# An eight-core streaming trunk rescheduled: narrower halo, packed weights, a stacked depthwise convolution, norms inside the stages

## Chip, cores and metric

The kernel runs on the 8 cores of one Trainium2 chip, each core working on half of one prompt and on one sample stream. The time is that of the slowest core, in device microseconds (us). Some executions fall into a slower state in which the cores of one die show a lower granted TensorE clock than the others (in the slowest run of the changed kernel, 4371.96 us, 0.844 to 0.853 on one die and 0.972 to 0.974 on the other); only fast runs are compared here, and where a profile fell into the slow state, a core of the undisturbed die is read and named. The engines are PE (TensorE; PEld its weight loads), DVE (VectorE), ACT (ScalarE), POOL (GpSimd) and SP (SyncE).

## The reference, cut to what matters

```python
def trunk(x, conv_past, ...):                 # D = 1024, 4 layers
    for i in range(DEPTH):
        h = rms_norm(x, norm_mix_g[i])
        if i % 2 == 0:   # gMLP: v normalised per token, mixed over chunks of 128 frames
            z = gelu(h @ w_in + b_in); u, v = z[..., :3072], layer_norm(z[..., 3072:])
            y = (u * (tril(w_s) @ v + b_s)) @ w_out + b_out
        else:            # GLU -> causal depthwise convolution, width 31 -> LayerNorm -> silu -> pointwise
            a = h @ w_pw1 + b_pw1; glu = a[..., :D] * sigmoid(a[..., D:])
            c = silu(layer_norm(depthwise(concat(past, glu)) + b_dw)); y = c @ w_pw2 + b_pw2
        x = x + y
        h = rms_norm(x, norm_ffn_g[i])
        x = x + (silu(h @ w_gate) * (h @ w_up)) @ w_down     # D_FF = 2816
    return rms_norm(x, norm_final_g), conv states, normalised v
```

Four prompts of 4096 frames and eight sample streams of 32 frames. All matmuls run in bf16 with f32 sums.

## The kernel before

Activations lie channels-first: 8 blocks of 128 channels by up to 1184 token columns, in three tiles of up to 416. A core makes two passes over all four layers. The core with the second half of a prompt recomputes the 256 frames before it, the halo. The norms form stages of their own, behind a barrier:

```python
def ffn(layer, tiles):
    P.barrier()
    norm_to_h(tiles, "ffng", layer)      # per tile: 8 squares (ScalarE), 8 ones-matmuls, rsqrt, 8 scalings (VectorE)
    for mb in range(11):
        ...                              # gate/up
    for m in range(KC):
        ...                              # down: all tiles of an output block, then the next block
```

The depthwise convolution multiplies by diagonal 128x128 matrices, which ScalarE builds for every tap, and leaves 7 of the 31 taps of seven channel blocks to VectorE:

```python
mms = [lambda e, k=k, ...: e.matmul(
    ps[:, b, 0:nm], lhsT=(DIAG7[:, k, :] if k < NDVE else DIAG[:, dp, k, :]),
    rhs=PD[:, kc, c0 + k:c0 + k + nm], start=(k == nd), stop=(k == 30)) for k in range(nd, 31)]
...
for k in range(nd):                      # NDVE = 7 taps
    ... P.op("dve", lambda e, ...: e.scalar_tensor_tensor(out=CC[:, kc, ...], in0=PD[:, kc, c0 + k:...],
            scalar=pcol("wdw", ...), in1=CC[:, kc, ...], op0=ALU.mult, op1=ALU.add), ...)
```

And in the gating unit TensorE goes from the v projection to u and mixing at once, so that mixing waits for all of v to be normalised.

## Time and profile before

| | before |
|---|---|
| fast runs | 4489 to 4492 us |
| TensorE busy, idle (core 5) | 4109.5, 379.5 us |
| VectorE, ScalarE busy | 2085.1, 1293.3 us |
| mean granted clock | 0.96 |

TensorE, busy 92% of the span and 83% of the chain that ended last, sets the time: the question for every part of the change is how many columns it takes out of TensorE's stream, and which of its gaps. The prediction shows the lines. One more table of stretches: the four convolutions of this kernel, from the first pointwise 1 matmul to the first FFN matmul (columns: stretch, length, busy time of PE, PEld, DVE, ACT, POOL with counts, granted clock, DMA share, GB/s).

```profile
659.60:879.10 219.50, 196.68 (x1247) 123.51 (x1245) 143.04 (x307) 123.09 (x309) 8.74 (x10) 0.94 0.25 32
1665.40:1865.30 199.90, 176.07 (x1248) 113.37 (x1246) 130.88 (x307) 117.74 (x309) 8.74 (x10) 0.93 0.27 33
2763.90:3016.40 252.50, 219.30 (x1446) 127.98 (x1444) 166.04 (x360) 129.19 (x310) 8.73 (x10) 0.93 0.23 31
3942.60:4196.80 254.20, 221.14 (x1445) 128.53 (x1444) 165.78 (x359) 129.16 (x310) 8.74 (x10) 0.93 0.21 27
```

They take 926.1 us together, of which TensorE is busy 813.2 and idle 113.

### The profile page before, as it was taken

Reading aid. Unit: us, or ns where it says so; the run is one execution under the profiler, and the core shown is the slowest. Engines: PE = TensorE matmul, PEld = TensorE weight load, DVE = VectorE, ACT = ScalarE, POOL = GpSimd, SP = SyncE. Lnnn points to the kernel's source line nnn. Section 1 sums busy time; section 2 is a strip of 40 time slices with the busy share of each in tenths; the row PEclk is TensorE's granted clock in tenths of the full one; section 3 lists DMA queues with packets and bytes.
Section 4 is the critical chain, followed back from the end, with each engine's and each line's share of the span. In section 5 each row is a group of like instructions: output and inputs, shape, how many; then the busy total and the mean of one; then the engine's idle time right before and its main releaser. Section 6 shows DMA issues by size and latency. Waiting matters only on the chain.

```text
span 4489.0 us, 71170 instructions; the slowest of 8 cores (4479.6 to 4489.0 us)
## 1 busy us (share of the span) xinstructions
PE 4109.5 (92%) x25674; PEld 2433.8 (54%) x25674; DVE 2085.1 (46%) x4066; ACT 1293.3 (29%) x2821; POOL 350.1 (8%) x372
## 2 busy tenths in 40 slices
PE   6899999799899999896899999979998999997998
PEld 2465656566466666563355555635544555554554
DVE  4764225622865226523776212762157652148422
ACT  3222225511322126412312222541032121146311
POOL 0000110011001110010000001001100001100000
PEclk9999999899999999898999999989999999998999
DMA  6344573267345563377334455115543445640345
GB/s 122 52 62 59 61 67 39 29 77 79 59 71 68 71 68 39 40 81 140 60 55 67 57 61 67 22 29 67 58 68 49 61 64 65 65 50 1 48 60 82
DMA packets 514118, 273.78 MB, mean 61 GB/s; under 512 B 192944, under 2 KB 508720, under 8 KB 513712
## 3 DMA queue, kind: packets, MB, share of 16 engines
q0 software_dynamic: 489216, 239.10, 44.2%
q1 hardware_dynamic: 24560, 30.14, 2.6%
q8 instruction: 213, 3.49, 0.3%
q14 instruction: 129, 1.06, 0.1%
HBM read 498.48 MB, written 9.80 MB: 113 GB/s over the span
## 4 chain that ended last, share of the span: by engine, by line
PE 83%; DVE 7%; ACT 5%; issue 3%; SPq 1%; DMA 1%; DVEq 0%; ACTq 0%
PE ps L387 29%; PE ps L401 15%; PE ps L451 9%; PE ps L616 8%; PE ps L551 7%; PE ps L673 6%; PE ps L779 5%; ACT SQ L52 4%; DVE BIG L810 2%; PE ps L833 2%; PE ps L572 1%; PE ps L340 1%; SPq L856 1%; DVE BIG L493 1%; DVE FT L582 1%
## 5 line engine op out<-in xcount | busy, mean ns | idle before, releaser
L387 PE MATMUL ps<-hA,RING 128*128 128x384 bf16 (+3 forms) x8448 | 1323.5, 320 | 0.0
L387 PEld LDWEIGHTS ps<-hA,RING 128*128 128x128 bf16 x8448 | 814.9, 98 | 509.5 <-issue 6.9
L394 DVE TENSOR_TENSOR BIG<-ps,FT 128x384 bf16<-128x384 f32 (+2 forms) x528 | 285.1, 541 | 991.3 <-PE ps L387 975.9
L401 PE MATMUL ps<-BIG,RING 128*128 128x384 bf16 (+2 forms) x4224 | 659.5, 319 | 0.0
L52 ACT ACTIVATE FT<-ps 128x384 f32<-128x384 f32 (+4 forms) x556 | 263.6, 477 | 1057.0 <-PE ps L387 1016.8
L401 PEld LDWEIGHTS ps<-BIG,RING 128*128 128x128 bf16 x4224 | 405.9, 98 | 252.3
L52 ACT ACTIVATE SQ<-xA 128x384 bf16<-128x384 f32 (+3 forms) x432 | 181.2, 498 | 819.8 <-DVE xA L405 633.4
L616 PE MATMUL ps<-AUX,RING 128*128 128x384 bf16 (+2 forms) x2304 | 380.9, 326 | 34.3 <-DVE AUX L594 33.2
L551 PE MATMUL ps<-hA,RING 128*128 128x384 bf16 (+2 forms) x2304 | 395.0, 329 | 3.6 <-DVE FT L582 3.6
L451 PE MATMUL ps<-RING,hA 128*128 128x512 bf16 (+1 forms) x1776 | 392.0, 383 | 6.8 <-DVE hA L354 6.8
L779 PE MATMUL ps<-BIG,AUX 128*128 128x384 bf16 (+2 forms) x2388 | 362.1, 313 | 0.7 <-ACT AUX L52 0.7
L405 DVE TENSOR_TENSOR xA<-ps,xA 128x384 f32<-128x384 f32 (+3 forms) x192 | 103.9, 541 | 554.3 <-PE ps L401 554.3
L52 ACT ACTIVATE AUX<-ps,PPS 128x384 bf16<-128x384 f32 (+2 forms) x288 | 165.0, 576 | 612.7 <-PE ps L551 560.3
L616 PEld LDWEIGHTS ps<-AUX,RING 128*128 128x128 bf16 x2304 | 223.8, 98 | 187.2 <-issue 50.5
L810 DVE SCALAR_TENSOR_TENSOR BIG<-BIG,PPS 128x384 f32<-128x384 bf16 (+2 forms) x588 | 301.1, 578 | 38.1 <-ACT BIG L52 38.1
L340 PE MATMUL ps<-SQ,ONES 128*128 128x384 bf16 (+3 forms) x432 | 131.7, 478 | 191.3 <-ACT SQ L52 191.3
L551 PEld LDWEIGHTS ps<-hA,RING 128*128 128x128 bf16 x2304 | 223.3, 99 | 143.6 <-issue 13.8
L451 PEld LDWEIGHTS ps<-RING,hA 128*128 128x128 bf16 (+1 forms) x1776 | 173.0, 99 | 226.0 <-issue 25.8
L779 PEld LDWEIGHTS ps<-BIG,AUX 128*128 128x128 bf16 x2388 | 222.9, 97 | 133.5 <-issue 2.1
L354 DVE SCALAR_TENSOR_TENSOR hA<-xA,PPS,FT 128x384 bf16<-128x384 f32 (+3 forms) x384 | 200.8, 601 | 119.7 <-ACT FT L52 119.7
L673 PE MATMUL ps<-hA,RING 128*128 128x384 bf16 (+2 forms) x1536 | 251.5, 328 | 0.0
L52 ACT ACTIVATE AUX<-IDENTB,PPS 128x128 bf16<-128x128 bf16 x796 | 241.1, 390 | 0.0
(72 smaller groups left out, 2695.7 us busy)
## 6 DMA issues: line engine op xcount, KB each, us to landing
RING<-ffn_w_gate POOLq DMA_DIRECT2D x88, 512.0 KB, 7.9
RING<-ffn_w_up POOLq DMA_DIRECT2D x88, 512.0 KB, 9.8
RING<-ffn_w_down POOLq DMA_DIRECT2D x64, 704.0 KB, 9.5
RING<-sgu_w_in POOLq DMA_DIRECT2D x24, 1024.0 KB, 11.6
RING<-sgu_w_in POOLq DMA_DIRECT2D x32, 768.0 KB, 7.9
RING<-sgu_w_out POOLq DMA_DIRECT2D x32, 768.0 KB, 7.6
RING<-conv_w_pw POOLq DMA_DIRECT2D x32, 512.0 KB, 9.3
RING<-conv_w_pw POOLq DMA_DIRECT2D x8, 1024.0 KB, 10.2
```

The lines of the kernel that those rows point to most:

```text
L52: return self.e.activation(**kw)
L340: P.op("pe", [lambda e, kc=kc, n=n, par=par, b=b: e.matmul(ps[:, b, 0:n], lhsT=ONES[:, :], rhs=SQ[:, par, kc, 0:n], start=(kc == 0), stop= ...
L354: P.op("dve", lambda e, kc=kc, c0=c0, n=n, par=par, tt=tt: e.scalar_tensor_tensor(out=out_fn(kc, tt, c0, n), in0=xA[:, kc, c0:c0 + n], sca ...
L387: P.op("pe", [lambda e, kc=kc, w_=w_, b_=b_, c0=c0, n=n, j=j: e.matmul(ps[:, b_, 0:n], lhsT=w_[:, kc, j * 128:(j + 1) * 128], rhs=hA[:, kc ...
L394: P.op("dve", lambda e, bu=bu, n=n, par=par, mc=mc, c0=c0: e.tensor_tensor(out=A_[:, mc, c0:c0 + n], in0=ps[:, bu, 0:n], in1=FT[:, 4 + par ...
L401: P.op("pe", [lambda e, kc=kc, b=b, c0=c0, n=n, sW=sW: e.matmul(ps[:, b, 0:n], lhsT=sW[:, kc, :], rhs=A_[:, kc, c0:c0 + n], start=(kc == 0 ...
L451: P.op("pe", [lambda e, kc=kc, b=b, cc0=cc0, rows=rows, wv=wv: e.matmul(ps[0:rows, b, :], lhsT=hA[:, kc, cc0:cc0 + rows], rhs=wv[:, kc, :] ...
L551: P.op("pe", [lambda e, kc=kc, b=b, c0=c0, n=n, w_=wus[s], off=off: e.matmul(ps[:, b, 0:n], lhsT=w_[:, kc, off:off + 128], rhs=hA[:, kc, c ...
L616: P.op("pe", [lambda e, kc=kc, b=b, c0=c0, n=n, w_=wos[s], off=off: e.matmul(ps[:, b, 0:n], lhsT=w_[:, kc, off:off + 128], rhs=UG[:, kc, c ...
L673: P.op("pe", [lambda e, kc=kc, w_=w_, b_=b_, c0=c0, n=n, j=j: e.matmul(ps[:, b_, 0:n], lhsT=w_[:, kc, j * 128:(j + 1) * 128], rhs=hA[:, kc ...
L779: mms = [lambda e, k=k, b=b, kc=kc, dp=dp, c0=c0, nm=nm, nd=nd: e.matmul(ps[:, b, 0:nm], lhsT=(DIAG7[:, k, :] if k < NDVE else DIAG[:, dp, ...
L810: P.op("dve", lambda e, k=k, kc=kc, c0=c0, nm=nm: e.scalar_tensor_tensor(out=CC[:, kc, c0:c0 + nm], in0=PD[:, kc, c0 + k:c0 + k + nm], sca ...
```

## The change

It is a new schedule of the same mathematics. The intent: fewer token columns (the prompt is split at frame 2078, so 30 extra frames replace the halo of 256), weights packed by the host so that a partition's row is contiguous, a depthwise convolution in which four taps and 32 channels share the 128 rows, norms folded into the stage before them, and the gating unit's mixing one head behind its u. A stack below is such a set of shifted copies of one channel block; the tail of a convolution is what follows its last depthwise block: LayerNorm, silu, pointwise 2 and the next norm. The core of the diff, cut:

```diff
-    ST_COLS = [(0, 1152), (1152, 1184)]
+TA = [(0, 384), (384, 384), (768, 288)]
+TB = {0: [(0, 384), (384, 384), (768, 256)], 1: [(0, 384), (384, 384), (768, 320)]}
 ...
+            def later(self, tt, c0, n, d1, d2):          # norm of a tile: sum after d1 groups, scaling after d2 more
+                if self.final is None:
+                    h_ready[tt] = False
+                after(d1, lambda: (self.sum(tt, c0, n), after(d2, lambda: self.scale(tt, c0, n))))
 ...
+            ws = [load(6), load(7)]                      # FFN: the last two output blocks tile by tile
+            for tt, (c0, n) in enumerate(tiles):
+                for j in range(2):
+                    down(6 + j, ws[j][1], ws[j][0], tt, c0, n)
+                    ...                                  # squares of the next norm
+                nnorm.later(tt, *nt, 1, 1)
 ...
+            after(2, v_norm)
+            for hd in range(4):
+                for i, (mc, tt) in enumerate(units):
+                    u_group(hd, mc, tt)
+                    if hd > 0:
+                        mix(hd - 1, mc, tt)
 ...
+            def stack(kc, eng="sp"):                     # row r*32+c holds channel q*32+c, shifted by r
+                for r in range(4):
+                    for q in range(4):
+                        P.dma(eng, lambda e, r=r, q=q: e.dma_start(
+                            out=STK.v[r * 32:(r + 1) * 32, i, q, 0:win],
+                            in_=PD.v[q * 32:(q + 1) * 32, kc, r:r + win]), ...)
+                for j in range(8):
+                    for q in range(4):
+                        mms.append(lambda e, j=j, q=q: e.matmul(
+                            ps[q * 32:(q + 1) * 32, b, 0:nm], lhsT=w[:, q * 8 + j, :],
+                            rhs=STK.v[:, i, q, c0 + 4 * j:c0 + 4 * j + nm], start=(j == 0), stop=(j == 7)))
```

## The prediction

> **What bounds the kernel now.** First the states. Four executions took 4978.88, 4490.53, 5246.91 and 4490.70 us; the profiled one is 4490.53, with all eight cores within 0.2% of one another at a mean clock of 0.96. I predict for that fast state, and core 5's trace is the one read. Then the page: TensorE is busy 92% of the span, VectorE 46%.
>
> ```profile
> PE 4109.5 (92%) x25674; PEld 2433.8 (54%) x25674; DVE 2085.1 (46%) x4066; ACT 1293.3 (29%) x2821; POOL 350.1 (8%) x372
> ```
>
> The chain that ended last says the same by line, and the list of TensorE's waits says where the other 380 us are.
>
> ```profile
> PE 83%; DVE 7%; ACT 5%; issue 3%; SPq 1%; DMA 1%; DVEq 0%; ACTq 0%
> ...
> PE ps L340 <- ACT SQ L52: 191.3, 54, 25.9
> PE ps L727 <- DVE SQ L714: 69.3, 8, 13.6
> PE ps L616 <- DVE AUX L594: 33.2, 34, 3.6
> PE ps L572 <- DVE BIG L493: 27.1, 7, 6.1
> ```
>
> The reader is to see two separate things: a stream of matmuls that only fewer or cheaper matmuls can shorten, and a few kinds of gap, the largest being the column sums of each RMS norm (line 340) waiting for ScalarE's squares.
>
> To split the two by stage I read the busy times in stretches that I cut at the stages (here of the first pass: a norm, gate/up of an FFN, pointwise 1 of the convolution, its depthwise part, its LayerNorm; columns: stretch, length, PE, PEld, DVE, ACT, POOL busy, clock, DMA share, GB/s).
>
> ```profile
> 371.00:386.00 15.00, 7.92 (x26) 3.27 (x27) 6.16 (x12) 12.34 (x27) 1.59 (x2) 0.64 0.56 72
> 386.00:559.00 173.00, 173.00 (x1058) 103.83 (x1057) 42.72 (x78) 34.62 (x70) 16.66 (x18) 0.99 0.54 58
> ...
> 659.60:723.00 63.40, 63.40 (x386) 37.86 (x384) 23.96 (x47) 15.21 (x25) 3.49 (x4) 0.98 0.40 51
> 723.00:808.00 85.00, 81.77 (x567) 54.79 (x565) 74.25 (x156) 64.01 (x201) 1.75 (x2) 1.00 0.12 14
> 808.00:854.00 46.00, 33.73 (x208) 21.39 (x209) 33.45 (x83) 32.49 (x56) 0.00 (x0) 0.85 0.00 1
> ```
>
> Dense stages are 100% TensorE at a clock of 0.98 to 1.00; the low mean comes from the gaps (0.64). So matmuls cost what their column count says. From the chain of waits in order of time: 1056 gate/up matmuls of 384 columns in 173.06 us, 163.9 ns each; taking that out of stages of mixed width, 256 columns are 108.1 ns and 416 are 176.3; 432 of 512 in 94.81 us are 219.5 ns; a 128-column one is 79 (66.2 us over 840). I interpolate 288 to 122.5 and 320 to 136.
>
> Adding the chain's stage starts over both passes gives the time before: loads with first norms 101, V projection with its LayerNorm gap 496 (of which PE work 392), gated part u/mix/out 806, FFNs 1980, pointwise 1 251, the rest of the convolutions up to the FFN 675, other norms 151, final norm and store 26. Sum 4486.
>
> [...] the present loads take 98 ns and lie hidden (PEld 54% beside a full PE). [...] "DMA" is 1% of the chain, so bigger pieces alone should buy little. [...]
>
> **The change part by part.** It is nearly a new schedule. I count both kernels' columns from their loop nests.
>
> Fewer token columns. The old one recomputes a 256-column halo in the second half; the new one splits the sequence at frame 2078 and needs 32 extra. FFN columns fall from 8832 to 8448. FFN after: each pass has one tile set 384+384+288 (450.3 ns for a set) and three of 384+384+256 (435.9) or 384+384+320 (463.8), times 528 matmuls per set: 1901 us (was 1980). V: 35 chunks of 128 tokens x 48 x 220 ns = 370, the sample now sharing its chunk (was 392). u and out: 384 matmuls per set = 691; mixing 24 x (32 x 79 + 3 x 60 ns) = 65; together 756. Pointwise 1: 128 per set = 230. Pointwise 2: 64 per set = 115. LayerNorm sums 16 per set = 29. Norm sums 8 per set for 18 norms = 64.
>
> Depthwise convolution. Before: per channel block 24 diagonal 128x128 matmuls, 7 more taps on VectorE (588 instructions, 301 us), 796 ScalarE instructions (241 us) that build diagonals; its TensorE work is 331+23+12+12 = 379 us. After: shifted copies of the input are stacked by DMA so that 4 taps x 32 channels fill the 128 rows; 8 steps x 4 column groups of 32 outputs. If the four run at once a step costs one matmul time: 64 per set = 115, plus 13 us for the sample columns. I don't expect full overlap, as each step also needs four weight loads and eight issues: [...] I take 170 (an estimate). VectorE loses 325 us with the 32-column remainders, ScalarE 241, against 64 weight builds of about 1.2 us on VectorE.
>
> The stacking traffic is 16 SBUF-to-SBUF DMAs per stack. SyncE's issues before took 0.43 to 0.62 us each, so a stack takes some 8 to 10 us to issue and 2 to 3 to land. The first three stacks have 20 to 30 us of pointwise and depthwise matmuls to hide behind; the single stack 6 about 13, and stack 7, issued from GpSimd after the last pointwise 1, about 8 against 13. I put 6 us of wait on each of four convolutions: 24.
>
> Gaps. Squares are now interleaved with the last matmuls before a norm, its scaling is deferred by a count of groups, barriers are gone, and the last two output blocks go tile by tile so that tile 0 is ready early. The old 15 us per norm boundary (about 14 of them) becomes about 2.5, from VectorE's backlog behind 8 scalings of 0.6: 35. The V gap (about 24 us x 4 before) disappears: all 18 u groups of the first head, 22 us of TensorE, cover 9 normalisations of 1.07 us. In the last out phase VectorE has 24 additions of 0.55 and 18 mixes of 1.15 us against 27 us of TensorE: 7 us late, x 4 = 28. The LayerNorm tail of the convolution stays close to VectorE's pace (62 us of it beside 55 of TensorE): 10 x 4 = 40. Start 45 (was 51), between passes 33 (was 50: store, load and three norms still come before the first V matmul), end 16 (was 26).
>
> Sum: FFN 1901 + V 374 + u/mix/out 756 + 28 + pointwise 1 230 + depthwise 170 + LayerNorm sums 29 + pointwise 2 115 + stack waits 24 + tail 40 + norm sums 58 (those of the first norms are in the loads) + boundaries 35 + ends 94 = 3854. Long rewrites carry waits that I can't list; I add 46: 3900 us, 13% less.
>
> **The rivals.** (1) Column groups don't overlap: 64 x 4 matmuls per set are 460 us plus the sample, some 300 more, about 4200. [...] (2) The stack DMAs become the bound of the convolution: about 37 MB of extra copies, sharing engines with weight loads; if a stack of two takes 40 us instead of 20, each convolution waits 40 to 60 us: about 4080. For it: 512 extra issues from one queue, in order. Against it: the depthwise stage used only 12% of the DMA engines. (3) The gaps reappear as VectorE waits: its busy time only falls from 2085 to roughly 1750 us in a shorter span, and all the gaps that I removed need it to keep up. Of my 3900 some 3635 are matmuls and 265 gaps; before has about 460 (380 idle, and some 80 by which the norm and LayerNorm sums, 132 and 46 us busy, are stretched over their column count). If half of those 195 us comes back, 4000. [...]
>
> **Range and chances.** The matmul saving (4110 us of TensorE busy to some 3690, stretched sums included) is counted, so even with all 380 us of idle time kept it is 4070. Column overlap is the largest single doubt, and all doubts but one push up. 3900, with 3790 to 4150. Faster by over 2% 0.97, within 2% 0.02, slower 0.01.
>
> **What would show it.** TensorE busy near 3700 us and 94% or more; FFN stages at 230 to 245 us each; waits of norm sums for ScalarE below 60 us in all; one depthwise block of a 384-column tile in 1.5 to 2 us (5 us means rival 1); waits of depthwise matmuls for DMA under 50 us (over 150 means rival 2); a mean clock above 0.96 as the gaps go. It is wrong if dense stages run below a clock of 0.95 in a fast run, or if weights arrive late, which the old chain does not show.

## The result

| | before | after |
|---|---|---|
| fast runs | 4489.29 to 4492.26 us | 3894.44 to 3898.57 us (7 runs) |
| ratio of fast runs | | 0.8676, interval 0.8667 to 0.8686 |
| TensorE busy | 4109.5 us | 3646.3 us |
| TensorE idle | 379.5 us | 249.4 us |
| mean clock | 0.96 | 0.97 |

A ratio is the mean time of one kernel's fast runs over that of the other's of the same rounds, so not quite the ratio of the medians. Of the 593 us between the two traces, 463 are TensorE work and 130 are gaps. The page after (core 2), first the engines, then the chain by engine:

```profile
PE 3646.3 (94%) x26325; PEld 2293.0 (59%) x26325; DVE 1724.4 (44%) x3432; ACT 1082.2 (28%) x2043; POOL 190.4 (5%) x332
...
PE 85%; DVE 4%; issue 3%; DMA 3%; ACT 2%; SPq 1%; POOL 1%; DVEq 0%; ACTq 0%; POOLq 0%
```

TensorE's list of waits after (line, what it waited for, us in total, times, longest):

```profile
PE ps L420 <- ACT SQ L54: 104.0, 15, 34.8
PE ps L922 <- DVE hA L914: 33.7, 8, 5.1
PE ps L894 <- DMA AUX<-BIG: 31.4, 8, 5.1
PE ps L735 <- DVE xA L451: 20.8, 43, 0.6
PE ps L894 <- issue: 15.2, 6, 4.2
PE ps L550 <- DVE WSM L536: 9.0, 4, 2.2
PE ps L382 <- DVE hA L436: 7.3, 6, 3.3
PE ps L382 <- ACT hA L54: 6.8, 25, 0.3
```

Line 420 is the column sum of an RMS norm, 922 that of the LayerNorm in the convolution, 894 the depthwise matmuls, 735 the out projection, 382 a first use of a freshly scaled tile. Of the 104 us of line 420, the timeline puts 38 before the first V matmul of the first pass and 37 between the passes (34.8+1.3+1.2+1.0, and 0.4+22.2+8.5+6.3); the other 28 lie in the four convolutions. None lie at the boundaries between FFN and mixer, where the old kernel spent 13 to 16 us each.

The convolutions after, in the same columns as above:

```profile
583.50:750.80 167.30, 139.56 (x1418) 88.85 (x1416) 80.39 (x177) 77.38 (x140) 11.41 (x22) 0.90 0.45 91
1493.60:1658.80 165.20, 136.97 (x1419) 87.91 (x1418) 77.17 (x162) 77.25 (x141) 11.46 (x22) 0.91 0.42 86
2480.90:2656.70 175.80, 144.14 (x1674) 91.28 (x1673) 84.26 (x188) 79.01 (x140) 11.13 (x22) 0.89 0.47 96
3454.90:3632.80 177.90, 147.37 (x1673) 91.80 (x1672) 86.41 (x195) 79.08 (x139) 11.12 (x22) 0.88 0.46 88
```

They take 686.2 us, TensorE busy 568.0, idle 118. So the convolutions gave up 245 us of TensorE work, but their gaps stayed at the same total (113 before, 118 after), although VectorE's load in them fell from 606 to 328 us. The kinds changed. By the waits of these stretches, LayerNorm sums held 71 us before and 34 after, norm sums 31 and 28, pointwise 2 (for the silus after) 11 and 7; 47 us are new, 31 for the DMAs of the stacks and 15 put down to "issue". The mean clock even fell, from 0.93 to 0.90.

Where the 593 us came from, by stages cut at the first matmul of each (sums over both passes; a boundary's norm counts to the stage before it):

| stage | before | after | saved |
|---|---|---|---|
| convolutions, with the norm that follows | 926 | 686 | 240 |
| FFNs, with the norm that follows | 2070 | 1938 | 132 |
| V and its normalisation | 496 | 383 | 113 |
| u, mixing, out, with the norm that follows | 868 | 776 | 92 |
| start, between the passes, end | 128 | 112 | 16 |

### The profile page after: what moved, and what is told of

The parts are those of the page before. It is cut to its first block, busy times and chain, and to the rows that moved or that the text cites. A ratio compares the mean times of both kernels' runs of the same rounds, so it can differ in the third digit from the quotient of the medians.

```text
span 3895.7 us, 71020 instructions; the slowest of 8 cores (3880.9 to 3895.7 us)
## 1 busy us (share of the span) xinstructions
PE 3646.3 (94%) x26325; PEld 2293.0 (59%) x26325; DVE 1724.4 (44%) x3432; ACT 1082.2 (28%) x2043; POOL 190.4 (5%) x332
## 2 busy tenths in 40 slices
DMA packets 83807, 311.96 MB, mean 80 GB/s; under 512 B 15824, under 2 KB 29008, under 8 KB 66000
## 4 chain that ended last, share of the span: by engine, by line
PE 85%; DVE 4%; issue 3%; DMA 3%; ACT 2%; SPq 1%; POOL 1%; DVEq 0%; ACTq 0%; POOLq 0%
PE ps L387 46%; PE ps L484 16%; PE ps L607 9%; PE ps L735 7%; PE ps L894 2%; PE ps L420 2%; PE ps L382 1%; DMA yT<-xA 1%; DMA AUX<-BIG 1%; DVE BIG L943 1%; DMA xA<-xT 1%; DVE xA L451 1%; ACT hA L54 1%; PE ps L691 1%; ACT SQ L54 1%
## 5 line engine op out<-in xcount | busy, mean ns | idle before, releaser
L387 PE MATMUL ps<-hA,RING 128*128 128x384 bf16 (+3 forms) x12672 | 1952.0, 314 | 0.0
L387 PEld LDWEIGHTS ps<-hA,RING 128*128 128x128 bf16 x12672 | 1232.6, 98 | 640.3 <-issue 13.6
L476 DVE TENSOR_TENSOR BIG<-ps,FT 128x384 bf16<-128x384 f32 x528 | 276.2, 524 | 964.2 <-PE ps L387 922.1
L484 PE MATMUL ps<-BIG,RING 128*128 128x384 bf16 (+3 forms) x4224 | 634.0, 313 | 0.0
L451 DVE SCALAR_TENSOR_TENSOR xA<-ps,xA 128x384 f32<-128x384 f32 (+3 forms) x480 | 243.2, 522 | 567.6 <-PE ps L484 515.5
L735 PE MATMUL ps<-AUX,RING 128*128 128x384 bf16 (+3 forms) x2304 | 359.6, 313 | 21.0 <-DVE xA L451 20.8
L607 PE MATMUL ps<-RING,hA 128*128 128x512 bf16 x1584 | 348.4, 382 | 0.0
L607 PEld LDWEIGHTS ps<-RING,hA 128*128 128x128 bf16 x1584 | 155.4, 98 | 189.4 <-issue 6.0
L54 ACT ACTIVATE AUX<-ps,PPS 128x384 bf16<-128x384 f32 (+3 forms) x288 | 155.9, 556 | 362.7 <-PE ps L387 317.3
L420 PE MATMUL ps<-SQ,ONESD 128*128 128x384 bf16 (+4 forms) x440 | 96.1, 333 | 107.0 <-ACT SQ L54 104.0
L703 DVE SCALAR_TENSOR_TENSOR FT<-ps,PPS,AUX 128x384 f32<-128x384 f32 (+1 forms) x288 | 163.7, 568 | 29.8 <-PE ps L691 23.2
L719 DVE TENSOR_TENSOR AUX<-FT,AUX 128x384 bf16<-128x384 f32 (+3 forms) x288 | 151.2, 525 | 51.4 <-DVE FT L703 36.9
## 6 DMA issues: line engine op xcount, KB each, us to landing
RING<-w_dn POOLq DMA_DIRECT2D x64, 704.0 KB, 6.4
```

The costliest lines, as they stand in the source:

```text
L54: return self.e.activation(**kw)
L387: P.op("pe", [lambda e, kc=kc: e.matmul(ps[:, b, 0:n], lhsT=aps[kc], rhs=hA[:, kc, c0:c0 + n], start=(kc == 0), stop=(kc == KC - 1)) for k ...
L420: P.op("pe", lambda e, kc=kc: e.matmul(ps[:, b, 0:n], lhsT=ONESD[:, :], rhs=SQ[:, kc, 0:n], start=(kc == 0), stop=(kc == KC - 1)), reads=[ ...
L451: P.op("dve", lambda e: e.scalar_tensor_tensor(out=xA[:, m, c0:c0 + n], in0=ps[:, b, 0:n], scalar=bias, in1=xA[:, m, c0:c0 + n], op0=ALU.a ...
L476: P.op("dve", lambda e, bu=bu, n=n, f=f, mc=mc, c0=c0: e.tensor_tensor(out=A_.v[:, mc, c0:c0 + n], in0=ps[:, bu, 0:n], in1=FT[:, f, 0:n], ...
L484: P.op("pe", [lambda e, kc=kc: e.matmul(ps[:, b, 0:n], lhsT=w[:, kc, :], rhs=A_.v[:, kc, c0:c0 + n], start=(kc == 0), stop=(kc == 21)) for ...
```

## The experiments

The prediction held, so the runs ask whether for its reasons. Twelve kernels ran, all edits of the changed kernel. "Fast" below is the range of an experiment's fast runs; the changed kernel's is 3894 to 3899 us, and a signed number is against its median, 3897. The changed kernel itself was not run again beside the experiments; the kernel before was, and its fast runs there took 4491 to 4495 us, so differences of a few us mean nothing.

**1. Column groups in turn.** The four column groups of the depthwise convolution no longer alternate.

```diff
-                for j in range(8):
-                    for q in range(4):
+                for q in range(4):
+                    for j in range(8):
```

> The same depthwise matmuls in another order: all 8 steps of one column group of 32 before the next group, so that neighbours in the queue use the same columns. Theory A (the four column groups run at once): one block of a 384-column tile goes from 1.25 us to about 5 us, the depthwise matmuls from about 140 to about 490 us in all, the kernel +300 to +400 us, about 4250 us. Rival B (the matmuls are short for another reason, such as 32 output columns, and neighbours need not differ): within 30 us of the changed kernel. Besides: if the 4 us gaps that TensorE shows within the first depthwise blocks without a releaser come from its instructions arriving too slowly, they vanish here, as the same instructions are spread over four times the time.

Fast 3953 to 3957 us: +58, neither theory's number. The timeline of TensorE's matmuls shows why (start, length, line, shape, count). First the changed kernel, two channel blocks of three tiles:

```profile
640.20 7.23 PE L894 MATMUL ps<-AUX,BV 128*32 128x384 bf16 x192
```

then the same blocks with the groups in turn, and a seam between one block and the next, which read different weights (AUX or AUX,BV):

```profile
644.16 14.55 PE L894 MATMUL ps<-AUX,BV 128*32 128x384 bf16 x190
...
688.59 1.17 PE L894 MATMUL ps<-AUX,BV 128*32 128x384 bf16 x11
689.44 0.34 PE L894 MATMUL ps<-AUX 128*32 128x384 bf16 x1
689.60 0.33 PE L894 MATMUL ps<-AUX,BV 128*32 128x384 bf16 x1
689.61 0.33 PE L894 MATMUL ps<-AUX 128*32 128x384 bf16 x1
689.76 0.33 PE L894 MATMUL ps<-AUX,BV 128*32 128x384 bf16 x1
689.77 0.33 PE L894 MATMUL ps<-AUX 128*32 128x384 bf16 x1
```

A block takes twice as long (14.55 us against 7.23), not four times. At the seam the last group of one block and the first of the next run side by side, a pair every 0.16 us, although the program has all of the former ahead of the latter. So the records of this run still show two groups at once, and a third order was needed to see none.

**2. One column group.** All 32 matmuls of a block add into the same 32 output rows (a wrong result).

```diff
-  ps[q * 32:(q + 1) * 32, b, 0:nm], ... start=(j == 0), stop=(j == 7)
+  ps[0:32, b, 0:nm], ... start=(j + q == 0), stop=(j + q == 10)
```

> All 32 depthwise matmuls of a block add into the same 32 output rows, so they all use one column group, in the old order (a wrong result on purpose). The order experiment before gave 2.4 us per block, not 5, and its trace shows two neighbouring groups side by side at the seams of blocks. Theory A (one group takes one matmul at a time[...]): 5 us per block of 384 columns, about 430 to 490 us of depthwise matmuls in all, the kernel +240 to +340 us, about 4190 us. Rival B (a 32-column matmul takes half the time of a full one by itself): 2.4 us per block, about 3955 us, as in the order experiment.

Fast 4118 to 4119 us: +221, just below theory A's range.

```profile
629.70 27.96 PE L894 MATMUL ps<-AUX 128*32 128x384 bf16 x192
657.50 27.95 PE L894 MATMUL ps<-AUX,BV 128*32 128x384 bf16 x192
```

192 matmuls in 27.96 us against 7.23 is 3.87 times, so the alternating order overlaps the four groups almost fully. Within a group a matmul takes 146 ns for 341 columns on average, the price of a full one (163.9 ns for 384 columns in the dense stages of before, so also 146 for 341). Rival B is ruled out. The depthwise matmuls of line 894 took 451 us here and 141 in the changed kernel, 311 more, but the kernel only 221 more: TensorE's idle time fell from 249 to 179 us, since the stacks' waits vanished and those of the LayerNorm sums fell to 13 us. That is the first sign that the gaps in the convolution belong to other engines' pace. The gaps that are put down to "issue" vanish in both orders (0.3 and 0 us against 15.2), as the expectation of run 1 has it for instructions that come too slowly. The trace of the changed kernel points the same way. On its eight cores it has 31 such gaps of over 1.5 us, at nearly the same places of TensorE's stream, and each ended 1.25 to 1.75 us after a 16 KB packet of the instruction queue had landed (on core 2, packets at 632.94 and 1542.48 us, matmuls again at 634.52 and 1543.78). That TensorE waited for its own instructions there is an inference; no run changes their fetching alone.

**3. Norms after their stage.** Barriers and separate norm stages return; the FFN's last two blocks go block by block.

```diff
+            def whole(self, tiles):
+                flush()
+                P.barrier()
+                for tt, nt in enumerate(tiles):
+                    for kc in range(KC): self.square(kc, tt, *nt)
+                    self.sum(tt, *nt); self.scale(tt, *nt)
-                nnorm.later(tt, *nt, 1, 1)        # in the FFN; likewise in the gating unit and the convolution
+            nnorm.whole(ntiles)
```

> Only the norms are put back: squares, sums and scalings of all tiles come after the stage and a barrier, and the last two output blocks of the FFN go block by block again. Theory A (interleaving is worth what the boundaries of before cost): 14 boundaries go from 2 or 3 us back to about 15, so +150 to +220 us, about 4080 us, and the waits of norm sums for ScalarE's squares rise from 104 to about 250 us. Rival B (most of the boundaries' gain came from other parts, as packed weights or early loads): less than +60 us.

Fast 4027 and 4029 us: +132, near theory A and clear of B, but its waits rose only to 151 us. The profile fell into the slow state, so this is core 6 of the undisturbed die (span 4025.1). The page's first line and the norm sums here, and the norm sums of the changed kernel:

```profile
PE 3718.5 (92%) x26290; PEld 2297.0 (57%) x26325; DVE 1736.6 (43%) x3432; ACT 1030.5 (26%) x2015; POOL 192.2 (5%) x332
...
L420 PE MATMUL ps<-SQ,ONESD 128*128 128x384 bf16 (+4 forms) x440 | 162.5, 412 | 159.2 <-ACT SQ L54 150.9
```

```profile
L420 PE MATMUL ps<-SQ,ONESD 128*128 128x384 bf16 (+4 forms) x440 | 96.1, 333 | 107.0 <-ACT SQ L54 104.0
```

Idle time rose by 57 us (4025.1 - 3718.5 = 306.6 against 249.4) and busy time by 72, nearly all of it in the same 440 norm sums (162.5 against 96.1 us), which here stand behind gaps: eight of 384 columns took 3.37 us there (at 345.7 and 592.2 us), against 1.46 within a dense stretch of the changed kernel (at 1881.0 us). The changed kernel has the same 3.37 us between its passes, where the granted clock was 0.50 (1897 to 1931 us; 1.00 at 1881). So over half of what the gaps of this run cost (72 of 129 us) is booked as busy time, and a list of waits misses it.

**4. Mixing in its own head.** v is normalised at once, and a head's mixing stands beside its own u.

```diff
-            after(2, v_norm)
+            v_norm()
-                    u_group(hd, mc, tt)
-                    if hd > 0:
-                        mix(hd - 1, mc, tt)
+                    u_group(hd, mc, tt)
+                    if tt == 2:
+                        for t_ in range(3): mix(hd, mc, t_)
```

> Only the order in the gating unit is put back: v is normalised at once, and each head's mixing stands beside its own u groups, with its out groups after. Theory A: four gaps of 20 to 24 us come back, and the lateness of VectorE in the last out phase (predicted as 7 us each) goes, so +50 to +100 us. Rival B (the gap was caused by the waits on row sums and broadcast constants, which are now early): less than +20 us.

Fast 3976 to 3979 us: +81, theory A. TensorE's new wait stands in its list, for the normalisation of v:

```profile
PE ps L691 <- DVE BIG L650: 60.8, 12, 12.7
```

**5 and 6. Small pieces of weights.** The first try split the same contiguous rows into 16 (`nsp = 16`).

> Weight loads keep their packed layout but are cut into 16 pieces per partition row instead of 2, so a piece is 512 B or less as it was before. Theory A (weights arrive early enough anyway): within 1%, 3860 to 3940 us, although a load takes longer to land and GpSimd longer to issue it (0.5 to about 1.1 us). Rival B (the large pieces carry part of the gain): +60 us or more, with TensorE's waits for the ring appearing in the list of waits.

It tested nothing: its only fast run took 3903.64 us, but the trace shows the same 83,807 DMA packets as the changed kernel, so pieces that lie side by side at both ends had been joined. The second try has the host lay the weights out so that a row really is in 16 pieces.

```diff
-  w_gu = din("w_gu", [DEPTH, 11, 128, 4096])
+  w_gu = din("w_gu", [DEPTH, 11, 16, 128, 256])          # and so for all seven
-  in_=src.rearrange("p (a n) -> p a n", a=nsp)
+  in_=src.rearrange("a p n -> p a n")
```

> The earlier try at small pieces changed nothing: its trace has the same 83,807 DMA packets, because pieces that lie side by side on both sides are joined. Here the weights lie in the memory so that a partition's row is really cut into 16 pieces of 512 B or less as stored (as before). Packets should rise to about 500,000 and the weight queue's share from 35% to about 45%. Theory A (weights arrive early enough anyway): within 1%, 3860 to 3940 us. Rival B (DMA engines that are busier with weights delay the stacking DMAs and the loads at the ends): +20 to +80 us, in waits of depthwise matmuls for DMA and at the ends.

Three of its four runs were slow; the fast one took 3894.37 us, and in the slow runs the cores of undisturbed dies took 3884 to 3894 us. The DMA lines, first of this run (its profile is of a slow execution of 4011 us), then of the changed kernel:

```profile
DMA packets 590687, 311.96 MB, mean 78 GB/s; under 512 B 277968, under 2 KB 569680, under 8 KB 590288
...
q0 software_dynamic: 546944, 243.66, 50.8%
```

```profile
DMA packets 83807, 311.96 MB, mean 80 GB/s; under 512 B 15824, under 2 KB 29008, under 8 KB 66000
...
q0 software_dynamic: 40064, 243.66, 35.2%
```

Seven times the packets and a share of the DMA engines that is 44% larger cost nothing, although a 1 MB gate/up load landed in 10.2 us (in the slow execution) against 8.4: theory A. The size of the pieces took no part in the gain.

**7. Without the last two stacks** (a wrong result).

```diff
-            stack(6)
-            stack(7, "pool")
```

> The stacking DMAs of the last two channel blocks of each convolution are left out (a wrong result on purpose: the matmuls read the stacks of two earlier blocks). The list of waits puts 31 us on these DMAs. Theory A (they are on the path): -25 to -45 us. Rival B (the LayerNorm behind them is bound by VectorE, which catches up while TensorE waits): less than -12 us, and the waits of LayerNorm sums for VectorE grow instead.

One fast run, 3868.49 us, and undisturbed dies at 3845 to 3870: -28, theory A. The waits of depthwise matmuls for DMA fell from 31.4 to 3.7 us; those of the LayerNorm sums stayed (36.7 us). Over all eight cores the stretches around the convolutions, from the end of one FFN's down to the start of the next FFN's, fell from 1311.5 to 1278.5 us in the mean.

**8. Half the LayerNorm on VectorE** (wrong: no subtraction of the mean).

```diff
-                for op, f in ((ALU.subtract, 0), (ALU.mult, 1)):
+                for op, f in ((ALU.mult, 1),):
```

> The subtraction of the mean is left out of the LayerNorm of the convolution (a wrong result on purpose): 96 of VectorE's 0.52 us instructions, 50 us of its time, all within the tails of the four convolutions. Theory A (the tail goes at VectorE's pace): -35 to -55 us. Rival B (the tail is bound by latencies between ScalarE, VectorE and TensorE): -5 to -20 us.

Fast 3861 to 3890 us, median 3864: -33, just short of theory A's range and clear of B's. (The check still calls the result correct; it does not feel this mean.) VectorE lost 41 us of busy time (1724.4 to 1683.3) and the kernel 33: in the tail TensorE goes mostly at VectorE's pace. The gain lies where the edit is: the stretches around the convolutions fell by 34 us in the mean of the eight cores (1311.5 to 1277.1). In the list of waits little of it stands under VectorE's name: within the convolutions the norm sums' waits for ScalarE's squares fell from 28 to 8 us and those of pointwise 2 for ScalarE's silu from 7 to none, as those squares and silus come after the additions and multiplications on VectorE. (Over the whole kernel the norm sums' waits fell by only 14 us, 104.0 to 89.7, since those at the ends were 6 us longer on the core read.)

**9. Block 5 before block 6.** All tiles of depthwise block 5 come before the wait for stack 6.

> All three tiles of depthwise block 5 are computed before block 6 is asked for, so 2.4 us more matmuls stand ahead of the wait for the last two stacks in each convolution. If the wait for the stacks is on the path: -6 to -10 us. If VectorE's pace in the tail sets the end: within 3 us.

Fast 3895 to 3899 us, the same as the changed kernel. The wait for the stacks fell by 7 us (31.4 to 24.3) and came back behind it, where the work moved forward is missing: the LayerNorm sums waited 3 us longer (36.9), pointwise 2 for the silus 3 (9.9) and the norm sums in the convolutions 1 (29.0), though differences of this size also occur between cores. The stretches around the convolutions are the same in the mean of the cores (1311.5 and 1311.9 us). An account that fits runs 7 and 9 both, and that no run tests by itself, is that the tail begins when the last stack lands, whatever TensorE does until then. Reordering TensorE's work did not help here; leaving out the transfers did.

**10 to 12. The ends, and a faster version.** The final norm writes to an idle buffer, so that loading x for the second pass need not wait for the store of the first, and V starts tile by tile.

```diff
-  out, wk = xA[:, kc, c0:c0 + n], [("x", kc, tt)]          # final norm in place
+  out, wk = YO.v[:, kc, c0:c0 + n], YO.keys(kc, c0, n)
-            for tt in range(3):
-                first_norm(p, n0, tt, *TA[tt])             # all norms, then V
+            first_norms(n0, ...)                           # sum and scaling of a tile when V asks for it
```

> The final norm writes to a buffer of its own that is idle then, so the loads of the second pass no longer wait for the stores of the first; at each start a tile's V matmuls follow its own norm instead of all norms; the second and third weight load wait for the first tiles of x. Expected: the stretch between the passes from 47 to about 30 us, the first V matmul from 49 to about 40 us, together -20 to -30 us. Rival: the stores and loads share the DMA engines and the memory, so that the same bytes take the same time and less than -8 us is won.

Fast 3920 and 3921 us: +24, a miss in the wrong direction (read on core 5, of an undisturbed die). At the start the first V matmul did come at 27.5 us instead of 49.1, but the next tile's then waited 17 us for its scaling. Between the passes x did not land earlier (the first squares ran at 1915 us in both kernels), and the bias of the first V chunk, queued behind x and the stores, now landed only at 1939 us; VectorE sat idle for 14.8 us before the addition that needs it, with the scaling of the next tile behind that in its program. The mended version loads the bias first and puts the stores behind the loads:

> As the earlier try at the ends, but its two faults are mended: the bias that the first V chunk needs is loaded ahead of x, and the stores of the first pass go behind the loads of the second. Expected: the x tiles land one after the other about 7 us apart, the stretch between the passes goes from 47 to about 25 us, the first V matmul from 49 to about 35 us with small waits behind it; together -20 to -35 us, 3863 to 3878 us. Rival: the bytes at the ends set the time whatever their order, less than -8 us.

Fast 3887 to 3896 us: -8, hardly more than its rival allows, and one of its three fast runs (3895.85) lies in the changed kernel's range. The two stretches named did become as short as expected: on core 0 the first V matmul came at 28.9 instead of 49.8 us, and from the last down matmul to the next V it took 26 instead of 49. But from there to the FFN's down matmuls it took 24 us more in the first pass (475.7 against 452.1) and 16 more in the second, as V's matmuls now waited for the scalings of later tiles; the norm sum of the third tile began at 1937 us in both kernels. The stretch between the passes, of the changed kernel and of this one:

```profile
1890.00:1940.00 50.00, 12.60 (x53) 5.06 (x50) 17.71 (x36) 14.18 (x36) 0.53 (x1) 0.60 0.81 236
```

```profile
1890.00:1930.00 40.00, 15.41 (x60) 5.91 (x58) 16.80 (x34) 16.01 (x35) 0.53 (x1) 0.65 1.00 248
```

The DMA engines are 81% busy at 236 GB/s there, and 100% at 248 when nothing waits: so the bytes of x, y and the first weights very probably set when the last tile can begin, and an earlier first matmul only moved the wait. The last version adds GpSimd for three of eight mean subtractions:

```diff
-  P.op("dve", lambda e, ...: e.tensor_tensor(out=CC.v[:, kc, c0:c0 + n], ...
+  P.op("pool" if f == 0 and kc > 4 else "dve", lambda e, ...: e.tensor_tensor(out=CC.v[:, kc, c0:c0 + n], ...
```

> The same, and three of the eight mean subtractions of each LayerNorm tile in the convolution go to GpSimd. Leaving out all eight won about 35 us. If GpSimd's run beside VectorE's at up to 1 us each: another -5 to -15 us. Rival: GpSimd is slower than 2 us an instruction, or holds up the weight loads that queue behind it: the same or longer than without.

Fast 3867 to 3878 us, median 3873.7: -15 against the version without it, and a ratio of 0.862 (0.860 to 0.864) to before: the fastest correct kernel, 0.6% ahead of the changed one. A subtraction took GpSimd 950 ns against 521 on VectorE, and ran beside VectorE's copies of the same tail (at 701.9 to 704.8 us in the first convolution), before VectorE had come to the subtractions left to it. Over eight cores the stretches around the convolutions fell by 19 us against run 11.

## Why the prediction was right, point by point

3900 us was predicted and 3894 to 3899 measured. That closeness is partly luck: the terms were off by up to 54 us and cancelled. Grouped as the stages above (each group with its share of norm sums, 3.6 us, and boundaries, 2.5 us):

| terms | predicted | measured | off by |
|---|---|---|---|
| FFN (1901, 8 norms, 6 boundaries) | 1945 | 1938 | -7 |
| u, mixing, out (756 + 28, 4 of each) | 808 | 776 | -32 |
| V (the working gives 370, the sum took 374) | 374 | 383 | +9 |
| convolution (230+170+29+115+24+40, 4 of each) | 632 | 686 | +54 |
| start, between, end | 94 | 112 | +18 |
| allowance for unlisted waits | 46 | | -46 |

**TensorE's stream.** Counting columns and pricing them by dense stages was right: about 3690 us of busy time was predicted and 3646.3 measured. Most of the gain, 463 of 593 us, is this, as the prediction had it. Experiments 2 (the four-way overlap is real and worth 221 us) and 5/6 (packing is worth nothing) agree with its account.

**Mixing.** 79 ns per 128-column matmul was mis-sized: it divided the group's busy time, which includes a tail after each short group (0.33 us of records for three where the next group starts after 0.17), by its count. In the changed kernel three of them fit into 0.17 us between u groups, 57 ns each (start of line 691 to start of the next line 387):

```profile
170.38 0.33 PE L691 MATMUL ps<-WSM,BIG 128*128 128x128 bf16 x3
170.55 1.46 PE L387 MATMUL ps<-hA,RING 128*128 128x384 bf16 x8
171.85 0.33 PE L691 MATMUL ps<-WSM,BIG 128*128 128x128 bf16 x3
172.02 1.14 PE L387 MATMUL ps<-hA,RING 128*128 128x288 bf16 x8
```

With 57 ns, the 24 x 32 of them come to 44 us instead of 61, half of the group's error.

**Depthwise matmuls.** 170 us was the estimate for an overlap that is not full, which no trace of before could show; lines 894 and 900 show 148 busy us, at 3.87-fold. The weight loads that each step also needs did not prevent it: 192 matmuls with as many loads took 7.23 us. The weight builds on VectorE took 1.22 us each, as expected.

**The convolution's waits.** This is the term that was too small: 24 + 40 us of waits and 10 of boundaries were predicted, 118 us of idle time measured. The stacks took 31 us where 24 were expected, which was close (a SyncE issue took 0.60 us in the median, and in the first convolution TensorE went on at 671.31 us, 2.8 us after the last issue of stack 6 had ended), and run 7 shows them on the path. The 10 us per tail were the fault. The prediction set 62 us of VectorE beside 55 of TensorE, 7 apart, and put 10; it left out that norm sums, LayerNorm sums and silus each wait in turn for a chain over VectorE and ScalarE (28, 34 and 7 us; with 31 for the stacks and 15 of "issue" that is 115 of the 118), and that the granted clock is lower around such a wait (0.50 from 726.2 to 736.3 us, around one of 6.45 us that ended at 731.2; 0.90 over these stretches, 1.00 assumed). Of the group's 54 us, 44 are idle time and 10 busy time, the depthwise matmuls' 22 us gained set against 32 lost on the others. Runs 8 and 12 show that relieving VectorE there shortens the kernel. One part of the chain was overlooked by prediction and runs alike: within the first convolution's tail ScalarE loads an activation table seven times, 1.28 us each, two of them (at 685.1 and 704.0 us) between the variance and the reciprocal root that the scaling waits for. What fewer loads would gain, no run shows.

**Boundaries.** From about 15 to 2.5 us each was right in kind: no wait for squares is left between FFN and mixer. Run 3 gives 132 us for putting them back where 14 x 12.5 = 175 was expected.

**The V gap.** Run 4 gives 81 us for it, with the predicted lateness of VectorE set against it: 4 x 24 - 28 = 68 was expected.

**The ends.** 33 us between the passes was a guess from the order of instructions; 47.8 were measured (last down matmul at 1892.1 us, first V matmul at 1939.9), hardly less than the 50 before. Runs 10 and 11 point to the bytes, not the order, as the cause.

**The checks named in advance.** TensorE near 3700 us and 94% busy: yes, 3646 and 94%. FFN stages of 230 to 245 us: yes, 242 with their norms. Clock above 0.96: yes, 0.97; dense stages stayed at 0.98 to 1.00. Depthwise waits for DMA under 50 us: yes. Norm-sum waits under 60 us: no, 104, as the 75 at the ends had been overlooked. A depthwise block of a 384-column tile in 1.5 to 2 us: about 1.36, better (an estimate from 7.23 us for two blocks of three tiles, 384 of their 1024 columns). Rivals 1 and 2 did not come; of rival 3, the convolution's gaps stayed.

## What to carry to other kernels

Price a matmul stage by its columns at the rate of the kernel's own dense stages (about 3690 us predicted here, 3646 measured), and take the cost of a short matmul from start to start (57 ns here), not from busy time over count (79). A gap can cost more than the list of waits shows, as the matmuls behind it ran slower here (eight norm sums in 3.37 us against 1.46): 129 us for 57 of idle time in run 3, though in the changed convolutions only some 32 us beside 118 idle. When a stage sheds load from two engines, look for the dependency chain between them before counting its gaps as gone: here the convolution lost 245 us of matmuls, and its gaps came to as much as before.
